# A hybrid decoder step on one core: full-height state products, alternating banks in the chained products, shared sums on two engines

## The chip, the cores and the metric

The kernel runs on one core of one Trainium2 chip. TensorE multiplies matrices out of SBUF into PSUM; VectorE, ScalarE and GpSimd work element by element, and GpSimd does not read PSUM here; transfers are issued by SyncE. The metric is device time in microseconds (us) of one execution, the median of three timed runs. One further execution was taken by the hardware profiler, and all rows below are from it.

## What is computed

One inference step of a two-layer decoder trunk for a prompt of 1,024 tokens, 8 samples of 8 new tokens each, and 16 meta tokens: 1,104 columns, which the kernel keeps with features on the partitions. Layer 0 is a Mamba-2 mixer and an MLP, layer 1 window attention and an MLP. Cut to what the change touches:

```python
# mixer, for each of 8 groups of heads; the samples' chunk is their 8 tokens
chunk_states = jnp.einsum('bclgn,bclgrp->bcgrpn', bb, decay_to_end[..., None] * xdt)
h_new = chunk_decay * h + chunk_states            # h: state_ssm, per sample
...
# MLP of either layer
h + jnp.square(jax.nn.relu(rmsnorm(h, norm_w) @ w_up)) @ w_down
```

All is float32. The kernel reaches that precision by splitting each operand in a rounded high part and the rest (hi and lo, type fp32r) and adding three products, hi·hi, hi·lo and lo·hi.

## The kernel before

**The planner.** The program is written as plain loops over tiles; a planner with a cost model of its own then sets the order of the instructions on each engine's queue and the semaphores. Each engine runs its queue in that order. So the order in the trace is not always that of the loops: where a tile's buffer is not free by the planner's reckoning, it moves another product's matmuls ahead.

**The mixer** (`mixer`, `group_in`, `ssd`; about 17 to 710 us). For each of 8 groups, `group_in` makes four projections of the normed input (`conv_mm`, through `mm3`, lines 179 to 181, into PSUM tiles `g`) for the group after, while `ssd` runs the present group's scan: first the chunk t = 8 (samples and meta tokens), then the prompt's eight chunks. At t = 8 the samples' states are brought forward. The 64 rows are the 8 samples' tokens. `bhl` holds B's hi parts in rows 0 to 63 and its lo parts in rows 64 to 127; `xh` holds x's hi parts in both halves; `bm` is `bhl` masked to one sample's rows, for each of 8 samples. Line 663 multiplies `bm` (128 rows) with `xh`, which gives hi·hi and lo·hi in one; line 664 adds hi·lo with the rows 0 to 63 of `bm` alone and `xl`, a tile of 64 rows from the ring `n1` of five buffers. Both have 256 columns. Line 665 adds two samples' PSUM tile `st` (one buffer) to the states. That is 8 samples in 8 groups, 64 instructions each of lines 663 and 664.

**The chained products** (`up_pair`, about 1,152 to 1,452 and 2,336 to 2,621 us; `down_blocks`, about 1,507 to 1,770 and 2,681 to 2,944 us). The MLP's inner blocks are multiplied by a scheme with seven products for each 2x2 block in place of eight. One chain is seven products; a product i is written in two halves of columns to a pair of PSUM banks, and its pair is named by `CHAIN[i]`, a letter of "adcbacd". There are four pairs, a to d, which is all of PSUM. After each product its pair is read out at once: in `down_blocks` by `tt(to, pv, to)` (line 1056, VectorE) into a target in SBUF. `up` runs 14 chains (f = 2 to 15) in each layer, `down_blocks` 16 (four blocks b, in each four parts p); the next chain begins again with a, then d. So the product 1 of a chain writes to the pair that product 6 of the chain before has left, with the one product 0 between them.

In `down_blocks` the target `uv` collects products that three results share. In the last block (b = 3), behind product 3, line 1081 adds `uv` to three of the four results (`hv[1][1]`, `hv[1][0]`, `hv[0][1]`), all on VectorE: 12 sums in each layer, recorded at line 1056, where `tt` is defined, as hh<-hh,us. Other work on VectorE in that stage: sums of weights (lines 986 and 992) and the lo parts of the next block's activations (line 1024, and line 966 for the block after the chains); on GpSimd the lo parts of the weights (line 856), of which a ring of six holds the parts of six products; on ScalarE the hi parts (lines 855 and 1023).

Of the kernel before, what the change touches and what calls it, by code (L numbers as in the profile page):

```python
# [8 lines left out]
F32 = mybir.dt.float32  # L9
F32R = mybir.dt.float32r  # L10
AF = mybir.ActivationFunctionType
ALU = mybir.AluOpType
# [4 lines left out]
P = 128  # L17
# [124 lines left out]
class Kernel:  # L142
# [180 lines left out]
    def mixer_consts(self, mp):  # L323
        nc, i = self.nc, self.i

        self.tri = mp.tile([P, P], F32, name="tri")
        self.tris = mp.tile([P, P], F32, name="tris")
        self.tri8 = mp.tile([80, 80], F32, name="tri8")
        self.tris8 = mp.tile([80, 80], F32, name="tris8")
        for tl, tls in ((self.tri, self.tris),):  # L330
            nc.gpsimd.memset(tl, 1.0)
            nc.gpsimd.affine_select(out=tl, in_=tl, pattern=[[1, P]], compare_op=ALU.is_ge, fill=0.0, base=0,
                                    channel_multiplier=-1)
            nc.gpsimd.memset(tls, 1.0)
            nc.gpsimd.affine_select(out=tls, in_=tls, pattern=[[-1, P]], compare_op=ALU.is_ge, fill=0.0, base=-1,
                                    channel_multiplier=1)
        for tl, strict in ((self.tri8, False), (self.tris8, True)):
            nc.gpsimd.memset(tl, 1.0)
            sv = tl[:, 0:64].rearrange("s (b q) -> s b q", q=8)
            mv = tl[:, 64:80]  # L340
            if not strict:

                nc.gpsimd.affine_select(out=sv, in_=sv, pattern=[[-8, 8], [0, 8]], compare_op=ALU.is_ge, fill=0.0,
                                        base=0, channel_multiplier=1)
                nc.gpsimd.affine_select(out=sv, in_=sv, pattern=[[8, 8], [1, 8]], compare_op=ALU.is_ge, fill=0.0,
                                        base=0, channel_multiplier=-1)
                nc.gpsimd.affine_select(out=mv, in_=mv, pattern=[[0, 16]], compare_op=ALU.is_ge, fill=0.0, base=-64,
                                        channel_multiplier=1)
                nc.gpsimd.affine_select(out=mv, in_=mv, pattern=[[1, 16]], compare_op=ALU.is_ge, fill=0.0, base=64,
                                        channel_multiplier=-1)  # L350
            else:

                nc.gpsimd.affine_select(out=sv, in_=sv, pattern=[[-8, 8], [-1, 8]], compare_op=ALU.is_ge, fill=0.0,
                                        base=-1, channel_multiplier=1)
                nc.gpsimd.affine_select(out=sv, in_=sv, pattern=[[8, 8], [0, 8]], compare_op=ALU.is_ge, fill=0.0,
                                        base=7, channel_multiplier=-1)
                nc.gpsimd.affine_select(out=mv, in_=mv, pattern=[[-1, 16]], compare_op=ALU.is_ge, fill=0.0, base=-65,
                                        channel_multiplier=1)

        self.bsel = mp.tile([P, NB], F32, name="bsel")  # L360
        nc.gpsimd.memset(self.bsel, 1.0)
        for h in range(2):
            bs = self.bsel[64 * h:64 * h + 64]
            nc.gpsimd.affine_select(out=bs, in_=bs, pattern=[[-8, 8]], compare_op=ALU.is_ge, fill=0.0, base=0,
                                    channel_multiplier=1)
            nc.gpsimd.affine_select(out=bs, in_=bs, pattern=[[8, 8]], compare_op=ALU.is_ge, fill=0.0, base=7,
                                    channel_multiplier=-1)

        self.cv = mp.tile([P, 32, 29], F32, name="cv")
        self.cvo = mp.tile([P, 32, 27], F32, name="cvo")  # L370
        nc.sync.dma_start(out=self.cv, in_=i["cv"])
        nc.scalar.mul(out=self.cv[:, :, 0:5], in_=self.cv[:, :, 0:5], mul=0.5)

        self.dcol = mp.tile([P, 16], F32, name="dcol")
        for h in range(2):
            nc.sync.dma_start(
                out=self.dcol[64 * h:64 * h + 64, :],
                in_=i["a_d_skip"].rearrange("o (t h) -> o h t", h=2)[:, h].broadcast_to([64, 16]),
                allow_slow_non_contiguous=True)
# [170 lines left out]
    def ssd(self, g, fm):  # L550
        nc, i, sp, ps = self.nc, self.i, self.sp, self.psa
# [4 lines left out]
        for t in [8] + list(range(8)):  # L556
# [6 lines left out]
            for h in range(2):  # L563
# [10 lines left out]
                                    in1=hb(self.dt[:n, t, 4 * g:4 * g + 4]), op=ALU.mult)  # L574
# [8 lines left out]
                                    op=ALU.mult)  # L583
# [19 lines left out]
            else:  # L603
# [3 lines left out]
                for b in range(NB):  # L607
                    e = SMP + 8 * b + 8
# [27 lines left out]
            if t == 8:  # L636
                nc.tensor.matmul(out=st[:, 0:256], lhsT=Bt[64:80, :], rhs=xd[64:80], start=True, stop=True)
                hT = sp.tile([P, 256], F32, tag="hT", bufs=2, name="hT")
                nc.vector.tensor_copy(out=hT, in_=st[:, 0:256])

                bhl = sp.tile([P, P], F32R, tag="bhl", bufs=1, name="bhl")
                nc.scalar.copy(out=bhl[:64], in_=Bt[:64])
                nc.vector.tensor_tensor(out=bhl[64:], in0=Bt[:64], in1=bhl[:64].bitcast(F32), op=ALU.subtract)
                xh = sp.tile([P, 256], F32R, tag="xh", bufs=1, name="xdh")
                xl = self.np.tile([64, 256], F32R, tag="n1", bufs=5, name="xdl")
                xdf = xd.rearrange("p h d -> p (h d)")
                nc.scalar.copy(out=xh[:64], in_=xdf[:64])
                nc.scalar.copy(out=xh[64:], in_=xdf[:64])
                nc.vector.tensor_tensor(out=xl, in0=xdf[:64], in1=xh[:64].bitcast(F32), op=ALU.subtract)
                bm = sp.tile([P, NB, P], F32R, tag="bm", bufs=1, name="bm")  # L650
                nc.gpsimd.tensor_tensor(
                    out=bm, in0=bhl.bitcast(F32).rearrange("p (o n) -> p o n", o=1).broadcast_to([P, NB, P]),
                    in1=self.bsel.rearrange("p (b o) -> p b o", o=1).broadcast_to([P, NB, P]), op=ALU.mult)
                hv = h0.rearrange("p b (h d) -> p b h d", d=64)
                for h in range(4):
                    nc.gpsimd.tensor_tensor(
                        out=hv[:, :, h], in0=hv[:, :, h],
                        in1=self.eendb[:, 4 * g + h].rearrange("p (b o) -> p b o", o=1).broadcast_to([P, NB, 64]),
                        op=ALU.mult)
                for b2 in range(4):  # L660
                    sps = ps.tile([P, 2, 256], F32, tag="st", name="st")
                    for b in range(2):
                        nc.tensor.matmul(out=sps[:, b], lhsT=bm[:, 2 * b2 + b], rhs=xh, start=True, stop=False)
                        nc.tensor.matmul(out=sps[:, b], lhsT=bm[:64, 2 * b2 + b], rhs=xl, start=False, stop=True)
                    nc.vector.tensor_tensor(out=h0[:, 2 * b2:2 * b2 + 2], in0=h0[:, 2 * b2:2 * b2 + 2], in1=sps,
                                            op=ALU.add)
                nc.sync.dma_start(out=self.o["ssm_s"][g], in_=h0)
            else:
                nc.tensor.matmul(out=st[:, 0:256], lhsT=Bt, rhs=xd, start=True, stop=True)
                hN = sp.tile([P, 256], F32, tag="hT", bufs=2, name="hT")  # L670
                nc.gpsimd.tensor_tensor(out=hN.rearrange("p (h d) -> p h d", d=64),
                                        in0=hT.rearrange("p (h d) -> p h d", d=64),
                                        in1=hb(self.eend[:, t, 4 * g:4 * g + 4]), op=ALU.mult)
                nc.vector.tensor_tensor(out=hN, in0=hN, in1=st[:, 0:256], op=ALU.add)
                hT = hN
# [80 lines left out]

    CHAIN = "adcbacd"

    def entry(self, big, h_d, w):

# [115 lines left out]
    def up_pair(self, layer, f, rd, rt):  # L878
# [8 lines left out]
        r = self.rx.tile([P, 4, n], F32, tag="rx", bufs=1, name="rx")  # L887

        for i, (wh, wl) in enumerate(self.up_weights(layer, f)):
            b = self.CHAIN[i]  # L890
            first = b not in banks
            if first:
                banks[b] = self.pq.tile([P, 1024], F32, tag=b, bufs=1, name="m" + b)
# [105 lines left out]
    def down_blocks(self, layer, rd, rt, R0, big, c0, chs):  # L999
# [58 lines left out]
        for b in range(4):  # L1058
            for p in range(4):
# [1 line left out]
                hv = [[h[j][i][:, p] for i in range(2)] for j in range(2)]  # L1061
                uv = us[:, p]
                for i, (wh, wl) in enumerate(self.down_weights(layer, b, p)):
                    e = self.CHAIN[i]
                    new = e not in banks
                    if new:
                        banks[e] = pq.tile([P, 1024], F32, tag=e, bufs=1, name="m" + e)
# [8 lines left out]
                        nc.scalar.copy(out=uv, in_=pv)  # L1076
                    else:
                        tt(to, pv, to)
                    if i == 3 and b == 3:
                        for to in (hv[1][1], hv[1][0], hv[0][1]):  # L1080
                            tt(to, to, uv)
                    step(b, p, i)


# [724 lines left out]
```

## Time and profile before

| | us |
|---|---|
| three timed runs, median | 3007.4 |
| their least and greatest | 3004.56, 3008.47 |
| the profiled execution | 3013.72 |
| its span, from the first to the last instruction | 3012.0 |

The profiled execution is 6.3 us longer than the median of the timed runs, and 1.7 us of it lie outside the span. In the span TensorE is busy for 2876.1 us, VectorE for 1963.2, ScalarE for 1453.5, GpSimd for 1397.4. Matmuls are pipelined: one's recorded duration overlaps the next, so what a matmul costs is read from the distance between two starts. A wait is listed with the instruction that waited and the one that released it; "issue" is idle time without a releaser.

### The profile page before, as it was taken

How to read it: one execution, taken by the hardware profiler on the slowest of the kernel's cores; microseconds unless marked ns; L12 is line 12 of the kernel's file. 1: busy time of each engine (PE TensorE's matmuls, PEld its weight loads, DVE VectorE, ACT ScalarE, POOL GpSimd, SP SyncE). 2: the span in 40 equal slices, each digit the busy share in tenths (PEclk: the TensorE clock that was granted, in tenths of full speed). 3: DMA queues.
4: the chain of work that ended last, by engine and by line, in shares of the span. 5: the costliest groups of instructions: out<-in, count | busy, mean ns of one | idle time of the engine just before them, and what ended most of it. 6: DMA issues, size and time to landing. Idle time of an engine off the chain costs nothing.

```text
span 3012.0 us, 50781 instructions
## 1 busy us (share of the span) xinstructions
PE 2876.1 (95%) x19750; PEld 2743.4 (91%) x19750; DVE 1963.2 (65%) x3172; ACT 1453.5 (48%) x2770; POOL 1397.4 (46%) x1231
## 2 busy tenths in 40 slices
PE   5999999999999989999999999999998999999998
PEld 4988898878999989999999999887878999999998
DVE  5777877876565575544467666776779555366675
ACT  5455555545444565444333326556564454433333
POOL 4456665654232305444255555445442544435552
PEclk8999999999999999999999999999998999999998
DMA  3244444445222223444643312223223434443432
GB/s 125 75 112 117 119 120 116 119 133 155 68 69 68 82 79 129 144 145 139 239 142 131 116 50 60 69 71 102 72 94 103 160 131 154 173 176 130 136 101 74
DMA packets 197545, 346.37 MB, mean 115 GB/s; under 512 B 28648, under 2 KB 130920, under 8 KB 194728
## 3 DMA queue, kind: packets, MB, share of 16 engines
q1 hardware_dynamic: 197304, 343.13, 35.7%
q8 instruction: 155, 2.54, 0.3%
q14 instruction: 86, 0.70, 0.1%
HBM read 252.92 MB, written 91.12 MB: 114 GB/s over the span
## 4 chain that ended last, share of the span: by engine, by line
PE 45%; DVE 9%; ACT 4%; issue 3%; POOL 2%; DMA 2%; SPq 0%; DVEq 0%; POOLq 0%; ACTq 0%
PE g L179 3%; PE g L180 3%; PE g L181 3%; PE mc L179 3%; PE mc L181 3%; PE mc L180 3%; PE md L181 3%; PE md L180 3%; PE md L179 3%; PE ma L179 3%; PE ma L181 3%; PE ma L180 3%; PE mb L179 1%; PE mb L180 1%; PE mb L181 1%
## 5 line engine op out<-in xcount | busy, mean ns | idle before, releaser
L179 PE MATMUL g<-S,w 128*128 128x384 f32 (+3 forms) x1656 | 561.3, 339 | 17.5 <-DVE hh L726 4.8
L165 POOL TENSOR_TENSOR w<-raw,w 128x1024 fp32r<-128x1024 f32 x140 | 348.4, 2491 | 475.1 <-ACT w L164 408.1
L180 PE MATMUL g<-S,w 128*128 128x384 f32 (+3 forms) x1656 | 562.8, 340 | 3.6 <-DVE S L319 3.0
L181 PE MATMUL g<-S,w 128*128 128x384 f32 (+3 forms) x1656 | 557.5, 337 | 1.8 <-POOL w L165 1.8
L856 POOL TENSOR_TENSOR w<-s,w 128x384 fp32r<-128x384 f32 (+1 forms) x240 | 326.5, 1363 | 367.0 <-ACT w L855 355.2
L856 POOL TENSOR_TENSOR w<-raw,w 128x384 fp32r<-128x384 f32 (+1 forms) x180 | 222.8, 1240 | 268.0 <-ACT w L855 251.9
L179 PEld LDWEIGHTS g<-S,w 128*128 128x128 f32 (+1 forms) x1656 | 315.1, 190 | 26.2 <-issue 5.9
L180 PEld LDWEIGHTS g<-S,w 128*128 128x128 f32 (+1 forms) x1656 | 315.1, 190 | 10.6 <-DVE S L319 4.1
L181 PEld LDWEIGHTS g<-S,w 128*128 128x128 f32 (+1 forms) x1656 | 315.2, 190 | 8.0 <-issue 3.3
L855 ACT CAST w<-s 128x384 fp32r<-128x384 f32 (+1 forms) x240 | 134.4, 562 | 211.3 <-PE ma L181 69.9
L179 PE MATMUL ma<-S,w 128*128 128x276 f32 (+1 forms) x736 | 212.9, 289 | 5.0 <-DVE us L1056 5.0
L180 PE MATMUL ma<-S,w 128*128 128x276 f32 (+1 forms) x736 | 212.5, 289 | 1.1 <-DVE S L820 0.9
L181 PE MATMUL ma<-S,w 128*128 128x276 f32 (+1 forms) x736 | 212.4, 289 | 0.0
L164 ACT CAST w<-raw 128x1024 fp32r<-128x1024 f32 x140 | 146.5, 1046 | 126.5 <-PE g L180 62.1
L534 DVE SCALAR_TENSOR_TENSOR fm<-xp,cv,fm 128x1024 f32<-128x1024 f32 x96 | 165.4, 1724 | 31.8 <-ACT fm L515 31.2
L855 ACT CAST w<-raw 128x384 fp32r<-128x384 f32 (+1 forms) x180 | 100.6, 561 | 164.0 <-PE md L181 77.3
L726 DVE TENSOR_TENSOR hh<-hh,g 128x384 f32<-128x384 f32 (+2 forms) x264 | 134.1, 530 | 68.8 <-PE g L181 68.3
L179 PE MATMUL md<-S,w 128*128 128x276 f32 (+1 forms) x464 | 135.5, 292 | 8.9 <-DVE hh L1056 8.7
L179 PEld LDWEIGHTS ma<-S,w 128*128 128x128 f32 x736 | 138.6, 188 | 5.7 <-ACT w L855 3.6
L180 PEld LDWEIGHTS ma<-S,w 128*128 128x128 f32 x736 | 138.7, 188 | 1.6 <-DVE S L820 1.1
L181 PEld LDWEIGHTS ma<-S,w 128*128 128x128 f32 x736 | 138.5, 188 | 0.0
L179 PE MATMUL mc<-S,w 128*128 128x276 f32 (+1 forms) x464 | 134.7, 290 | 3.9 <-DVE hh L1056 2.6
(462 smaller groups left out, 8846.6 us busy)
## 6 DMA issues: line engine op xcount, KB each, us to landing
raw<-in_w_up_dram SPq DMA_DIRECT2D x64, 512.0 KB
raw<-in_w_in_dram SPq DMA_DIRECT2D x48, 512.0 KB
raw<-in_w_downs_dram SPq DMA_DIRECT2D x64, 384.0 KB
ab<-acs_d SPq DMA_DIRECT2D x64, 256.0 KB
S<-t_d SPq DMA_DIRECT2D x18, 828.0 KB
S<-t_e SPq DMA_DIRECT2D x18, 816.0 KB
t_d<-rx SPq DMA_DIRECT2D x12, 1104.0 KB
t_e<-rx SPq DMA_DIRECT2D x12, 1088.0 KB
```

What stands on the lines that cost most here:

```text
L164: nc.scalar.copy(out=wh, in_=raw)
L165: nc.gpsimd.tensor_tensor(out=wl, in0=raw, in1=wh.bitcast(F32), op=ALU.subtract)
L179: mm(out=out, lhsT=wh, rhs=xh, start=(first and k == 0), stop=False)
L180: mm(out=out, lhsT=wh, rhs=xl, start=False, stop=False)
L181: mm(out=out, lhsT=wl, rhs=xh, start=False, stop=(k == n - 1))
L534: nc.vector.scalar_tensor_tensor(out=acc[:, :SEQ], in0=xp[:, k:k + SEQ], scalar=cv[:, j, k:k + 1], in1=acc[:, :SEQ], op0=ALU.mult, op1=ALU ...
L726: nc.vector.tensor_tensor(out=hv, in0=hv, in1=pt[:, :n], op=ALU.add)
L855: nc.scalar.copy(out=t[:, 0], in_=src)
L856: nc.gpsimd.tensor_tensor(out=t[:, 1], in0=src, in1=t[:, 0].bitcast(F32), op=ALU.subtract)
```

## The change

Three things change. (1) `xl` becomes a tile of 128 rows that is made once, with zeros in rows 64 to 127; the 64 rows of lo parts are written to its upper half in each group, and line 664's product takes all 128 rows of `bm` and `xl`. (2) `CHAIN` becomes two strings, "adcbacd" for even f or p and "abcdacb" for odd ones: the pairs b and d change places from chain to chain. (3) In the last block of `down_blocks`, the three sums with `uv` are made behind products 3, 4 and 5 in place of all behind 3; the first two, for `hv[1][1]` and `hv[0][1]`, are on GpSimd, the third, for `hv[1][0]`, on VectorE.

```diff
+        self.xl = mp.tile([P, 256], F32R, name="xdl")
+        nc.vector.memset(self.xl[64:].bitcast(F32), 0.0)
...
-                xl = self.np.tile([64, 256], F32R, tag="n1", bufs=5, name="xdl")
+                xl = self.xl
...
-                nc.vector.tensor_tensor(out=xl, in0=xdf[:64], in1=xh[:64].bitcast(F32), op=ALU.subtract)
+                nc.vector.tensor_tensor(out=xl[:64], in0=xdf[:64], in1=xh[:64].bitcast(F32), op=ALU.subtract)
...
                         nc.tensor.matmul(out=sps[:, b], lhsT=bm[:, 2 * b2 + b], rhs=xh, start=True, stop=False)
-                        nc.tensor.matmul(out=sps[:, b], lhsT=bm[:64, 2 * b2 + b], rhs=xl, start=False, stop=True)
+                        nc.tensor.matmul(out=sps[:, b], lhsT=bm[:, 2 * b2 + b], rhs=xl, start=False, stop=True)
...
-    CHAIN = "adcbacd"
+    CHAIN = ("adcbacd", "abcdacb")
...
-            b = self.CHAIN[i]
+            b = self.CHAIN[f % 2][i]
...
-                    e = self.CHAIN[i]
+                    e = self.CHAIN[p % 2][i]
...
-                    if i == 3 and b == 3:
-                        for to in (hv[1][1], hv[1][0], hv[0][1]):
-                            tt(to, to, uv)
+                    if b == 3 and i in (3, 4, 5):
+                        e, to = ((nc.gpsimd, hv[1][1]), (nc.gpsimd, hv[0][1]), (nc.vector, hv[1][0]))[i - 3]
+                        e.tensor_tensor(out=to, in0=to, in1=uv, op=ALU.add)
```

## Rows read from the trace of the kernel before

**Rows 1.** The page's first line and its part 1: the span, and of each engine the busy time, its share of the span and the count of instructions.

```profile
span 3012.0 us, 50781 instructions
...
PE 2876.1 (95%) x19750; PEld 2743.4 (91%) x19750; DVE 1963.2 (65%) x3172; ACT 1453.5 (48%) x2770; POOL 1397.4 (46%) x1231
```

**Rows 2.** Busy time by stretch: the mixer without its ends, the mixer's last group, the chained down products of layer 0, the chained down products of layer 1. Columns: from and to in us, length, then for each engine busy us and the number of instructions, the granted TensorE clock as a share of full speed, the DMA share, GB/s.

```profile
100.00:650.00 550.00, 545.25 (x3576) 489.26 (x3575) 433.88 (x717) 289.09 (x683) 340.72 (x417) 1.00 0.45 118
650.00:710.00 60.00, 49.43 (x313) 39.58 (x313) 43.79 (x90) 32.41 (x75) 36.16 (x37) 0.91 0.43 107
...
1507.00:1770.00 263.00, 253.86 (x1965) 251.55 (x1963) 178.49 (x203) 91.72 (x134) 141.03 (x109) 0.99 0.35 117
...
2681.00:2944.00 263.00, 253.68 (x1993) 251.68 (x1991) 177.40 (x203) 93.99 (x138) 138.63 (x109) 0.99 0.36 122
```

**Rows 3.** The longest of TensorE's waits in the mixer, 100 to 650 us: who waited for whom, us in total, times, longest one.

```profile
PE st L663 <- POOL bm L651: 2.0, 2, 1.0
```

**Rows 4.** TensorE's instructions in order of time, in group 0 (146 to 149 us) and in group 7 (from 680 us): start, duration, engine, line, operation, out and in, rows*columns of the weights, shape of the moving operand, count. How far apart two starts are is what one matmul costs the engine; the durations overlap.

```profile
146.48 0.32 PE L181 MATMUL g<-S,w 128*128 128x336 f32 x1
146.72 0.38 PE L664 MATMUL st<-xdl,bm 64*128 64x256 f32 x1
147.04 0.38 PE L663 MATMUL st<-xdh,bm 128*128 128x256 f32 x1
147.35 0.38 PE L664 MATMUL st<-xdl,bm 64*128 64x256 f32 x1
147.66 0.42 PE L179 MATMUL g<-S,w 128*128 128x336 f32 x1
...
148.23 0.34 PE L179 MATMUL g<-S,w 128*128 128x384 f32 x1
148.40 0.33 PE L180 MATMUL g<-S,w 128*128 128x384 f32 x1
...
680.62 0.38 PE L664 MATMUL st<-xdl,bm 64*128 64x256 f32 x1
680.94 0.66 PE L596 MATMUL y<-dec,xdt 128*64 128x128 f32 x8
```

**Rows 5.** The same view inside a product of the second layer's up stage.

```profile
2400.35 0.29 PE L180 MATMUL ma<-S,w 128*128 128x272 f32 x1
2400.48 0.29 PE L181 MATMUL ma<-S,w 128*128 128x272 f32 x1
```

**Rows 6.** All matmuls of line 664: count, least, median and greatest duration in ns, first and last start in us, form.

```profile
L664 PE MATMUL st<-xdl,bm x64: 377/381/388, 146.7 to 680.6; 64*128 64x256 f32 x64
```

**Rows 7.** TensorE's waits in the chained down products of layer 0 (the first four rows), of layer 1 (the next two) and in the up products of layer 0 (the last; the same view of layer 1's up products, 2336 to 2625 us, has no row).

```profile
PE md L179 <- DVE hh L1056: 3.7, 2, 2.3
PE ma L179 <- DVE us L1056: 3.2, 2, 1.6
PE mc L179 <- DVE hh L1056: 1.3, 2, 0.6
PE g L179 <- DVE hh L1056: 0.9, 1, 0.9
...
PE md L179 <- DVE hh L1056: 5.0, 2, 2.7
PE ma L179 <- DVE us L1056: 1.7, 2, 1.1
...
PE mc L179 <- DVE rx L885: 1.4, 1, 1.4
```

**Rows 8.** TensorE's instructions in order of time where the last block (b = 3) of layer 0's chained down products begins, and then the same place of layer 1; in brackets the idle time before one and what ended it.

```profile
1708.89 0.40 PE L179 MATMUL md<-S,w 128*128 128x276 f32 x1 [2.30 <-DVE hh L1056]
...
1712.31 0.43 PE L180 MATMUL md<-S,w 128*128 128x276 f32 x1
1712.54 0.43 PE L181 MATMUL md<-S,w 128*128 128x276 f32 x1
...
1716.62 0.36 PE L179 MATMUL md<-S,w 128*128 128x276 f32 x1 [1.36 <-DVE hh L1056]
...
2881.41 0.39 PE L179 MATMUL md<-S,w 128*128 128x272 f32 x1 [2.32 <-DVE hh L1056]
...
2889.41 0.36 PE L179 MATMUL md<-S,w 128*128 128x272 f32 x1 [2.69 <-DVE hh L1056]
```

**Rows 9.** Busy time by stretch, as in rows 2, for two short stretches after those waits.

```profile
1708.90:1712.70 3.80, 3.80 (x18) 3.80 (x19) 3.80 (x3) 0.00 (x0) 2.75 (x2) 0.57 0.00 0
...
2889.40:2893.70 4.30, 4.29 (x23) 4.30 (x24) 4.30 (x9) 1.03 (x2) 1.50 (x2) 0.62 0.00 0
```

**Rows 10.** VectorE's instructions in order of time at the same place of layer 0 (b = 3 begins).

```profile
1692.15 1.88 DVE L1024 TENSOR_TENSOR A<-A 128x1656 fp32r<-128x1656 f32 x1 [0.81 <-ACT A L1023]
...
1717.50 2.18 DVE L1056 TENSOR_TENSOR hh<-hh,us 128x552 f32<-128x552 f32 x2
...
1726.93 0.73 DVE L1056 TENSOR_TENSOR hh<-md,hh 128x552 f32<-128x552 f32 x1 [1.55 <-PE md L181]
```

**Rows 11.** Instructions of lines 1056, 986 and 856 in layer 0's chained down products, columns as in rows 6.

```profile
L1056 DVE TENSOR_TENSOR hh<-hh,us x12: 716/729/1539, 1717.5 to 1764.7; 128x552 f32<-128x552 f32 x12
...
L986 DVE TENSOR_TENSOR s<-raw x28: 543/550/1376, 1513.7 to 1737.5; 128x384 f32<-128x384 f32 x28
...
L856 POOL TENSOR_TENSOR w<-s,w x61: 1004/1017/2658, 1506.4 to 1756.5; 128x384 fp32r<-128x384 f32 x61
```

## The prediction, made before the changed kernel was run

> **What bounds the kernel now.** I read the engine totals first: TensorE is busy for 95% of the span, VectorE for 65%, GpSimd for 46% [rows 1]. So an edit pays where it takes time out of TensorE's stream, and nowhere else unless it ends a wait of TensorE. Then I read the three places that the change touches, each by its own stretch [rows 2]. In the mixer TensorE is busy for 545.25 of 550 us, VectorE for 433.88, GpSimd for 340.72. Its longest wait there comes to 2.0 us in all [rows 3]. The reader is to see a stage that is nothing but TensorE's stream, with a fifth of VectorE's time left over. The mixer's last group is different: 49.43 of 60 us at a granted clock of 0.91, with no projections left to fill in. In the chained down products TensorE is busy for 253.86 and 253.68 of 263 us, so some 9 us in each layer are waits [rows 2].
>
> A busy TensorE is not one at its peak, so I read the distance between starts next. In a stream of equal shape, 272 columns take 0.13 us [rows 5] and 384 take 0.17 [rows 4]; on that line 256 columns take 0.12. Around line 664 they take 0.31 to 0.32: 146.72, 147.04, 147.35, 147.66 [rows 4]. The odd one there is the height: 64 rows of weights between neighbours of 128. Recorded durations hide it, 0.38 us for both lines. TensorE counts as busy all the while, so no list of waits shows it.
>
> Last, the waits of the chained products [rows 7]. The up products have one of 1.4 us in layer 0 and none in layer 1. In the down products TensorE waits for VectorE's read-outs: 3.7 us on pair d, 3.2 on a, 1.3 on c in layer 0, and 5.0 on d, 1.7 on a in layer 1.
>
> **Part 1, the full-height products.** Added: one memset of 64 rows by 256 at the start, beside loads; nothing waits for it but the first product of line 664, at 146.7 us [rows 6]. The write of `xl` on VectorE stays as it is. Its tile no longer takes one of five buffers of the ring n1, which can only free others. As `xl` is one tile now, its write in a group waits for line 664 of the group before, some 75 us past (seven groups from 146.7 to 680.6 [rows 6]). No column is added: line 664 streams 256 columns as before. What goes is the change of height on both sides of each line 664. There are 64 [rows 6], each with a way in and a way out at 0.31 in place of 0.12: 64 x 2 x 0.19 = 24.3 us. This is the upper bound. Some ways out lead to line 596, whose weights are 64 columns wide (680.62 to 680.94 [rows 4]); that is a change of shape of its own and stays in part. So I take 22 us of TensorE's stream.
>
> How much of it reaches the end? Seven of eight groups, 19.3 us, lie where TensorE is busy for 99% of the time. With the stage shorter by 19 us, VectorE would be busy for 434 of 531, 82%, still not the bound, though some of its reads will come due too late. I take 0.9 of it, 17.4 us. The last group's 2.8 us lie in the scan's serial chain, beside idle time; I take half, 1.4. Sum 18.8 us. Lower bound 10: half swallowed by VectorE and by the order that the planner now finds. Can the part cost time? Only if a product of 64 rows were cheaper where it stands, and rows 4 show none that is.
>
> The Trainium skill speaks on both sides of this. TensorEngine Tiling (Array Packing), Key Properties, says that going from one tiling mode to another drains TensorE; the rows' 0.31 us agree. The same page under When to Use Tiling counsels the reverse of this change, that contractions of at most 64 rows be run as half-height tiles, since two such tiles can run side by side. By that rule padding would throw time away; it is the fifth rival below.
>
> **Part 2, the pairs of banks.** In the chain's own order, product 1 of a chain needs the pair d that product 6 of the chain before has just left, with one product (18 matmuls of some 0.13, 2.3 us) for VectorE to read it out. Now product 1 takes the pair that product 3 of the chain before left, four products earlier; product 3 takes that of product 6, three products earlier. Within a chain nothing changes: a is used again after three products, c after two. So the shortest distance between chains goes from one product to two (product 4 to the next product 0).
>
> In the up products the planner has already moved other matmuls ahead and TensorE does not wait [rows 7], so I take 0 there, with -1.4 as the best.
>
> In the down products the waits on d are four: 2.30 and 1.36 us in layer 0, 2.32 and 2.69 in layer 1 [rows 8], all where b = 3 begins. The first of each is product 1 behind product 6, 4.6 us in all; it should go. The second is product 6 behind the read-out of product 1 in the same chain, 4.05 us; it comes earlier when product 1 does, but is not lifted by the new letters. Behind the waits the granted clock is 0.57 and 0.62 [rows 9], near the lower of the two levels (1.2 GHz), after TensorE had stood idle for 2.3 to 2.7 us: in layer 0, 17 distances in 3.65 us (1708.89 to 1712.54 [rows 8]) in place of 2.2, a loss of 1.4; in layer 1 a loss of about 1.3. Together 4.6 + 4.05 + 2.7 = 11.4 us. Against taking all of it: VectorE works without a break from 1692.15 until the idle 1.55 us before 1726.93 [rows 10], so a read-out that no longer blocks one product will be late for another. I take half, 5.5. At the end of the chains, the first product of the next block waits 0.9 us for the last read-out of d [rows 7], in either layer by my estimate; the last chain (p = 3) now ends on b. Which bank that product takes is not to be seen before; half of 1.8, 0.9. Part 2 is 6.4 us, between 0 and 11.4 + 1.8 = 13.2.
>
> **Part 3, the shared sums.** 24 sums at 0.73 us [rows 11] are on VectorE; 16 of them leave, 11.7 us. But VectorE is idle between read-outs for most of b = 3 (1.55 us before 1726.93 [rows 10]); only the first chain's two per layer fall into the busy run, where two took 2.18 us at 1717.50 [rows 10]. GpSimd has no such sum in the trace. Nearest is line 856, 384 columns in 1.00 us undisturbed and 2.66 at most [rows 11]; 552 columns would be 1.44 to 3.8. Queued behind a sum on GpSimd are the lo parts of later weights (line 856), and TensorE waits for these; the cover is the ring of six products' parts. Behind the sum for `hv[0][1]` waits VectorE's read-out of product 6, and with it its queue; the cover is products 4 and 5, 4.6 us. GpSimd is busy for 141.03 of 263 us [rows 2]. I take 0, between -2 (the busy run) and +3. The +3 comes from a neighbour on VectorE that is slowed: line 986 goes from 0.55 to 1.38 us [rows 11], 0.83 for each of the two sums in the first chain of either layer.
>
> Here a rule speaks against the change as well. SBUF — State Buffer, Who interferes with whom, in the Trainium skill: a VectorE instruction with two SBUF inputs and a GpSimd one that reads SBUF block each other, and the second waits for the whole of the first. Rows 11 agree, with 0.55 to 1.38 and 1.00 to 2.66. Sums from SBUF on GpSimd then still take VectorE's time.
>
> **The sum.** 18.8 + 6.4 + 0 = 25.2 us off. Against the profiled execution's 3013.7 us this gives 2988.5. That execution is 6.3 above the median; against the median of 3007.4 it is **2982**.
>
> **The rivals.**
> First, only the mixer pays: VectorE's busy run, not the banks, sets the waits of the down products. For it: 33 us without a break. 3007.4 - 18.8 = 2989.
> Second, both pay in full: 24.3 + 13.2 off, 2970. For it: TensorE's 99% in the mixer. Against it: the busy run.
> Third, the mixer's gain is mostly swallowed, because VectorE's and GpSimd's work comes due late when TensorE runs ahead (5 us are left): 3007.4 - 5 - 6.4 = 2996. Against it: 82% at most.
> Fourth, the change does not do what it says: the 0.31 us come from something else than the height, say from the change between operands, and stay. 3007.4 - 6.4 = 3001. Against it: the streams of rows 5 change operands in every matmul at 0.13.
> Fifth, a half-height product costs TensorE almost nothing beside its neighbours, and padded it costs its 0.12 us: 64 x 0.12 = 7.7 slower, less 6.4, 3009. Against it: the 0.31 us after each. It is the rule on half-height tiles above.
> Sixth, slower: GpSimd becomes the bound of the last block. One chain gives TensorE 7 x 18 x 0.126 = 15.9 us. GpSimd has seven of line 856 in it, at the stage's mean of 1.29 us (141.03 / 109 [rows 2]) 9.1, and two sums, 2.9: 12.0, which fits. It decides when line 856 takes over (15.9 - 2.9) / 7 = 1.86 us there. At 2.0 with sums of 3.8 it is 21.6, 5.7 too much in each of 8 chains: 3007.4 - 18.8 + 46 = 3035.
>
> **How the numbers follow.** What a measurement of this kernel can tell from no change is about 0.2%, 6 us: below 3001.4 is faster, above 3013.4 slower. Chances: forecast 0.46, only the mixer 0.20, both in full 0.10, mixer swallowed 0.10, no effect of the height 0.05, half-height cheaper 0.03, GpSimd the bound 0.06. The first four are faster, 0.86; the next two within, 0.08; the last slower, 0.06. The range ends at both bounds: 24.3 + 13.2 + 2 off gives 2968, and 10 off with nothing from the banks and 3 for the sums gives 3000.
>
> **What the profile after would show.** Starts of lines 663 and 664 some 0.12 us apart, the form of line 664 128*128, the stretch from the first projections to the last scan shorter by 17 to 20 us; the waits of md on hh at the start of b = 3 gone or below 1 us, the clock there at 1.00; the up stages as long as before within 2 us; hh<-hh,us on GpSimd at 1.4 to 2.7 us and no wait of VectorE on it. Wrong would be: starts still 0.3 apart, or VectorE waiting for GpSimd before product 6's read-out, or the planner's new order putting gaps into the up stages, which have none now.

## The result and the profile after

The changed kernel takes 2987.2 us, median of four runs (2977.05 to 2988.97), beside 3007.6 for the kernel before: a ratio of 0.9927, 95% interval 0.9903 to 0.9951. Timed once more beside the experiments, it came to 0.9912 (0.9896 to 0.9928). The forecast was 2982, so 0.9915. The profiled execution took 2977.05 us.

The page's first line and part 1 of the changed kernel, which answer to [rows 1]:

```profile
span 2975.3 us, 50874 instructions
...
PE 2842.1 (96%) x19750; PEld 2728.4 (92%) x19750; DVE 1956.7 (66%) x3157; ACT 1455.1 (49%) x2770; POOL 1424.9 (48%) x1247
```

The same number of matmuls; TensorE is busy for 34 us less, GpSimd for 27.5 more. Where the time came from is read by stage. Each time below is the distance between matmuls that mark a stage's ends in the profiled execution: the scan to the last start of the prompt's state product (line 669 before), the chained stages from the first to the last start of matmuls into the pairs a to d.

| us | before | after |
|---|---|---|
| start to the end of the scan | 708.5 | 686.8 |
| from there to the first up chain | 443.2 | 443.4 |
| up chains, layer 0 and layer 1 | 300.2, 305.5 | 301.1, 304.7 |
| down chains, layer 0 | 268.9 | 266.4 |
| end of these to the up chains of layer 1 (attention) | 555.4 | 545.1 |
| down chains, layer 1 | 265.0 | 263.6 |
| what follows them | 69.3 | 68.1 |

The scan gave 21.7 us, the down chains and what follows 5.1, the up chains nothing. The 10.3 us of the attention stage are not the change's: no instruction is changed there, and the granted clock differs from execution to execution. The stage in the busy time by stretch, of the kernel before and then of the changed one (the two numbers before the last two are the clock and the DMA share):

```profile
1769.00:2325.00 556.00, 519.56 (x3408) 475.45 (x3407) 416.36 (x925) 312.91 (x744) 269.50 (x220) 0.95 0.26 79
```

```profile
1746.00:2291.00 545.00, 508.49 (x3404) 464.59 (x3404) 417.39 (x926) 312.37 (x744) 271.04 (x220) 0.98 0.26 81
```

By the clock, 0.05 x 556 = 28 us of full speed are missing in the one and 0.02 x 545 = 11 in the other; not all of that is on the path. In a second profile of the changed kernel (e9) the stage took 553.1 us and the whole execution 2988.6. So some 26 of the 36.7 us between the two profiled spans are the change's own, and the rest is put down to the attention stage's clock.

TensorE's order of time in group 1 of the changed mixer, to be held against [rows 4]. Line 666 was 663, and 667 was 664:

```profile
212.91 0.34 PE L180 MATMUL g<-S,w 128*128 128x384 f32 x1
213.08 0.28 PE L666 MATMUL st<-xdh,bm 128*128 128x256 f32 x1
213.20 0.28 PE L667 MATMUL st<-xdl,bm 128*128 128x256 f32 x1
213.32 0.28 PE L666 MATMUL st<-xdh,bm 128*128 128x256 f32 x1
213.44 0.28 PE L667 MATMUL st<-xdl,bm 128*128 128x256 f32 x1
213.55 0.34 PE L181 MATMUL g<-S,w 128*128 128x384 f32 x1
```

The starts stand 0.12 us apart, where they stood 0.31. Summed over all 128 state products, the distance to the next start fell from 37.8 to 17.6 us.

That is not the whole gain, since a change of height also lengthened the matmul behind it. The kernel before, behind the last half-height product of group 0 in [rows 4]:

```profile
147.66 0.42 PE L179 MATMUL g<-S,w 128*128 128x336 f32 x1
147.92 0.31 PE L180 MATMUL g<-S,w 128*128 128x336 f32 x1
148.07 0.32 PE L181 MATMUL g<-S,w 128*128 128x336 f32 x1
```

The first of these takes 0.26 us to the next start, the second, of the same shape, 0.15. So I also summed TensorE's whole stream from the first state product to the end of the scan, without its idle time: 550.7 us before and 525.5 after. The clock has a part in this: TensorE stood at the 1.2 GHz level for 10.2 us of that stretch before and for 6.8 after. In e7 and e11, two runs described below with the same mixer, it stood there for 10.2 us as before, and the stream is 526.4 and 526.3. So at the same clock the stream shrank by some 24 us. The idle time in the stretch grew from 15.3 to 19.3 us.

The longest of TensorE's waits in the changed mixer, and then in the down chains of layer 0 and of layer 1, which answer to [rows 3, 7]:

```profile
PE st L666 <- POOL bm L654: 7.3, 4, 2.7
```

```profile
PE mb L179 <- DVE hh L1059: 3.3, 1, 3.3
PE ma L179 <- DVE us L1059: 2.2, 2, 1.3
...
PE mb L179 <- DVE hh L1059: 2.6, 1, 2.6
```

The reader is to see that the wait on pair d has become one on pair b: product 3 of the first chain of b = 3 now waits for the read-out of product 6 before it, which is on b. In both layers together 8.7 us on d have become 5.9 us on b. And in the mixer a small wait has grown, 2.0 to 7.3 us, for `bm`. What TensorE did around that wait on b:

```profile
1681.59 0.28 PE L181 MATMUL mc<-A,w 128*128 128x276 f32 x1
1685.16 0.57 PE L179 MATMUL mb<-A,w 128*128 128x276 f32 x1 [3.28 <-DVE hh L1059]
1685.52 0.43 PE L180 MATMUL mb<-A,w 128*128 128x276 f32 x1
1685.75 0.43 PE L181 MATMUL mb<-A,w 128*128 128x276 f32 x1
```

After 3.28 us of idleness the starts stand 0.23 apart in place of 0.13, as they did in [rows 8]. The sums on GpSimd, to be held against [rows 11]:

```profile
L1084 POOL TENSOR_TENSOR hh<-hh,us x16: 1357/1378/1694, 1694.8 to 2902.9; 128x552 f32<-128x552 f32 x8, 128x544 f32<-128x544 f32 x8
```

### The profile page after: what moved, and what is told of

Its sections match the earlier page's. It is cut to its first block, busy times and chain, and to the rows that moved or that the text cites. A ratio compares the mean times of both kernels' runs of the same rounds, so it can differ in the third digit from the quotient of the medians.

```text
span 2975.3 us, 50874 instructions
## 1 busy us (share of the span) xinstructions
PE 2842.1 (96%) x19750; PEld 2728.4 (92%) x19750; DVE 1956.7 (66%) x3157; ACT 1455.1 (49%) x2770; POOL 1424.9 (48%) x1247
## 4 chain that ended last, share of the span: by engine, by line
PE 46%; DVE 9%; ACT 4%; issue 3%; POOL 2%; DMA 1%; DVEq 0%; SPq 0%; POOLq 0%; ACTq 0%
PE g L179 4%; PE g L180 3%; PE g L181 3%; PE mc L179 3%; PE mc L181 3%; PE mc L180 3%; PE ma L179 3%; PE ma L180 3%; PE ma L181 3%; PE md L181 2%; PE md L180 2%; PE mb L179 2%; PE mb L180 2%; PE md L179 2%; PE mb L181 2%
## 5 line engine op out<-in xcount | busy, mean ns | idle before, releaser
L179 PE MATMUL mc<-S,w 128*128 128x276 f32 (+1 forms) x464 | 134.4, 290 | 2.7 <-DVE rx L888 1.4
L181 PE MATMUL mc<-S,w 128*128 128x276 f32 (+1 forms) x464 | 134.0, 289 | 0.0
```

What stands on the lines that cost most here:

```text
L179: mm(out=out, lhsT=wh, rhs=xh, start=(first and k == 0), stop=False)
L181: mm(out=out, lhsT=wl, rhs=xh, start=False, stop=(k == n - 1))
```

## The experiments

The theory: (1) TensorE pays about 0.19 us for each change between 64 and 128 rows of weights, 128 times, and these lie in its stream; (2) in the down chains VectorE's unbroken run sets the waits, and the letters of the banks choose where they fall; (3) the sums are covered. The main rival for (1): the gain comes from the buffer of the ring n1 that `xl` frees, and the order that the planner then finds. Edits are against the kernel before unless said otherwise; each kernel is timed beside the kernel before on the same chip. Ratios have their 95% interval; the stages, in us, are each from one profiled execution.

| run | ratio | scan | down chains, layer 0 and 1 |
|---|---|---|---|
| before | 1 | 708.5 | 268.9, 265.0 |
| changed kernel, again (e9) | 0.9912 (0.9896 to 0.9928) | 689.0 | 265.5, 263.3 |
| e1, part 1 alone | 0.9925 (0.9910 to 0.9939) | 686.8 | 268.5, 264.9 |
| e2, part 2 alone | 0.9964 (0.9951 to 0.9977) | 709.6 | 264.4, 263.2 |
| e3, part 3 alone | 0.9990 (0.9979 to 1.0001) | 710.9 | 271.1, 266.3 |
| e4, own tile of 64 rows | 1.0013 (1.0000 to 1.0025) | 717.7 | 271.4, 264.7 |
| e5, half of the changes of height | 0.9960 (0.9949 to 0.9972) | 697.4 | 270.8, 266.5 |
| e8, parts 1 and 2 | 0.9913 (0.9899 to 0.9927) | 691.7 | 265.0, 263.9 |
| e6, e8 and bm first | 0.9909 (0.9893 to 0.9926) | 680.8 | 272.4, 264.8 |
| e7, e8 and lo parts on GpSimd | 0.9918 (0.9901 to 0.9936) | 687.4 | 266.5, 266.1 |
| e11, e8 and lo parts late | 0.9903 (0.9889 to 0.9917) | 687.6 | 258.9, 260.5 |
| e12, e11 and bm first | 0.9893 (0.9874 to 0.9911) | 682.2 | 265.8, 262.1 |
| e13, e12 with the lo parts placed | 0.9870 (0.9853 to 0.9887) | 682.1 | 264.3, 260.2 |

The stages differ somewhat between executions of the same instructions: the scan ends at 686.8 to 691.7 us in the six profiles with the changed mixer that do not make `bm` first, and the down chains of layer 0 take 268.5 to 271.4 us in the four that leave them as they were.

**Each part alone.** e1, e2 and e3 are the three parts of the diff, one at a time.

> Part 1 alone on the kernel before: full-height tile with zeros, nothing else. Height theory (each change of height on TensorE costs about 0.19 us, 128 of them in TensorE's stream): the scan's end moves up by 19 to 23 us and the time falls by 18 to 22 us, most of the whole change's 20. Rival, the down products pay: the time falls by under 12 us and parts 2 and 3 hold the rest.

> Part 2 alone: the pairs b and d change places. If the banks set the waits: the wait of product 1 where b = 3 begins goes in both layers, 5 to 9 us faster with the clock kept. If VectorE's unbroken run sets them: the wait comes back on another pair within a product or two, 0 to 4 us faster. The mixer stays as before within 2 us in both.

> Part 3 alone: two of three shared sums on GpSimd. If they are covered: within 3 us of before. If VectorE's run is the bound at the start of b = 3: up to 3 us faster. If GpSimd becomes the bound of the last block: slower by 5 us or more, with VectorE or TensorE waiting for GpSimd there.

Part 1 alone ends the scan at 686.8 us, as the whole change does, and leaves every chained stage within 0.6 us. So the mixer's 21.7 us are part 1's. Part 2 alone takes 6.3 us out of the down chains and 1.2 out of what follows; by its ratio it is 10.9 us faster (6.9 to 14.8). TensorE's wait for the read-out of d is gone, and one stands on b. The order of time in e2, where b = 3 of layer 0 begins:

```profile
1706.16 0.37 PE L179 MATMUL mb<-A,w 128*128 128x276 f32 x1 [3.04 <-DVE hh L1056]
1706.37 0.29 PE L180 MATMUL mb<-A,w 128*128 128x276 f32 x1
1706.50 0.29 PE L181 MATMUL mb<-A,w 128*128 128x276 f32 x1
...
1713.07 0.40 PE L180 MATMUL md<-S,w 128*128 128x276 f32 x1 [1.52 <-DVE S L1024]
```

That is neither of the two expectations whole: the wait does come back, at product 3 in place of product 1 and longer, but the starts behind it are 0.13 us apart, at full clock, and d has no second one for a read-out (what ends the 1.52 us is a lo part, line 1024). By the stages the gain is 7.5 us, more than the 0 to 4 of the second expectation. Part 3 alone made the down chains 3.5 us longer in its profile, and its ratio does not tell it from no change; e5, which leaves these stages alone, has them 3.4 us longer, so this is no more than executions differ by. In no profile does VectorE wait for a sum on GpSimd.

**Height or buffer.** e4 takes `xl` out of the ring but leaves its height; e5 leaves ring and shapes and halves the changes of height.

```diff
+        self.xl = mp.tile([64, 256], F32R, name="xdl")
...
-                xl = self.np.tile([64, 256], F32R, tag="n1", bufs=5, name="xdl")
+                xl = self.xl
```

> The kernel before with the lo parts of x in a tile of their own, still of 64 rows, so that the ring of five buffers has one user less and the product keeps its height. Height theory: starts of lines 663 and 664 stay 0.31 us apart, time within 4 us of before. Ring theory (the gain of part 1 comes from the freed buffer and the order that the planner then finds): 10 us faster or more.

```diff
                     for b in range(2):
-                        nc.tensor.matmul(out=sps[:, b], lhsT=bm[:, 2 * b2 + b], rhs=xh, start=True, stop=False)
-                        nc.tensor.matmul(out=sps[:, b], lhsT=bm[:64, 2 * b2 + b], rhs=xl, start=False, stop=True)
+                        nc.tensor.matmul(out=sps[:, b], lhsT=bm[:, 2 * b2 + b], rhs=xh, start=(b == 0), stop=False,
+                                         skip_group_check=True)
+                    for b in range(2):
+                        nc.tensor.matmul(out=sps[:, b], lhsT=bm[:64, 2 * b2 + b], rhs=xl, start=False, stop=(b == 1),
+                                         skip_group_check=True)
```

> The kernel before with the four products of a pair of samples in another order: both of line 663, then both of 64 rows. The same instructions with the same shapes, but half of the changes of height (64 in place of 128). Height theory: 64 x 0.19, so 9 to 12 us faster, the scan's end earlier by as much. Rival, a product of 64 rows costs 0.31 us by itself whatever stands beside it: within 3 us of before.

The freed buffer alone gains nothing, 1.0013. Its scan is 9.2 us longer, and that is mostly the clock: over 100 to 650 us the granted clock is 0.98, where it was 1.00 [rows 2]. TensorE stood at the 1.2 GHz level for 17 us there, each time behind a wait for `bm`, which loses 8.5 us. The busy time by stretch of e4:

```profile
100.00:650.00 550.00, 542.73 (x3519) 488.08 (x3518) 414.48 (x698) 283.86 (x667) 336.42 (x410) 0.98 0.43 116
```

The planner's order did change, though: the wait for `bm` is 7.3 us in e4 too, so it comes with the own tile and not with the height. With half of the changes of height the scan ended 11.1 us earlier, and TensorE's stream in it, without idle time and with as much time at 1.2 GHz as before, is 538.8 us (550.7 before, some 526.4 with none). Halving the count halves the cost: 11.9 us for 64 changes, 24.3 for 128, 0.19 each. In e5's order of time two products of 64 rows side by side take 0.43 us to the next start, where each alone took 0.31, so the price is not the 64-row product's own:

```profile
146.15 0.50 PE L666 MATMUL st<-xdl,bm 64*128 64x256 f32 x2
146.58 0.42 PE L181 MATMUL g<-S,w 128*128 128x336 f32 x1
146.84 0.32 PE L179 MATMUL g<-S,w 128*128 128x336 f32 x1
146.99 0.32 PE L180 MATMUL g<-S,w 128*128 128x336 f32 x1
```

Here too the matmul behind them takes 0.26 us in place of 0.15. So a change of height lengthens both of its neighbours: by some 0.09 us the matmul in front of it (0.12 to 0.21 at the median for a state product) and by some 0.10 the one behind. A half-height product between two full ones has a change on either side, which makes its 0.31.

**What the parts make together.** e8 is the changed kernel with the sums as before; e9 is the changed kernel itself.

> The changed kernel without its part 3: full-height products and alternating pairs, the shared sums on VectorE as before. If the parts add up: the sum of parts 1 and 2 alone, 0.9885 to 0.9895 of before, and 2 to 4 us below the changed kernel, since part 3 alone made the down products longer by 3.5 us. If part 3 is neutral or helps once the banks alternate: the same as the changed kernel within 2 us, 0.9925 to 0.994.

> The changed kernel itself, on the chip and beside the runs that the next two are read against. Parts add up: 0.99 to 0.991 of before. As in its first timing: 0.9925 to 0.994. In its profile the time by stage again: scan about 687 us, chained down products about 266 and 264 us, attention between 545 and 555 us, with the granted clock of that execution.

0.9913 and 0.9912, with down chains of 265.0 and 263.9 us against 265.5 and 263.3: part 3 makes no difference once the banks alternate. Both ratios lie between the two ranges that were expected. The parts' ratios multiply to 0.9879, with an interval of some 0.0022 either way if the three are independent, and e9's interval begins at 0.9896. So that something is lost in the whole is not shown; by stage nothing is, 21.7 + 7.5 - 3.5 = 25.7 us for the parts beside some 26 for the whole.

**Which wait stands in the down chains.** e7 moves the lo parts of the block behind the chains (line 969 in these files) from VectorE's run to GpSimd; e11 keeps them on VectorE, but behind the read-outs.

```diff
-        nc.vector.tensor_tensor(out=lo, in0=lo.bitcast(F32), in1=hi.bitcast(F32), op=ALU.subtract)
+        (e or nc.vector).tensor_tensor(out=lo, in0=lo.bitcast(F32), in1=hi.bitcast(F32), op=ALU.subtract)
...
-                    self.block_parts(p - 1, R0)
+                    self.block_parts(p - 1, R0, nc.gpsimd)
...
```

> Parts 1 and 2, and the lo parts of the block behind the chains (four instructions in each layer, 1.3 to 2.1 us each, in VectorE's unbroken run where b = 3 begins) on GpSimd. If VectorE's run sets the waits there: the run is 5 to 7 us shorter and TensorE's wait on the pair b falls from 2.6 to 3.3 us to under 1.5 in both layers, 3 to 6 us below parts 1 and 2. If GpSimd's work in turn makes the weights' lo parts late, or its sharing with VectorE slows both: within 2 us or slower.

```diff
-                    self.block_parts(p - 1, R0)
+                    with self.tc.issue_after(self.last_read):
+                        self.block_parts(p - 1, R0)
                 if p == 3 and i == 5:
-                    self.block_parts(3, R0)
+                    with self.tc.issue_after(self.last_read):
+                        self.block_parts(3, R0)
...
-                        tt(to, pv, to)
+                        self.last_read = tt(to, pv, to).ins
```

> Parts 1 and 2, and the lo parts of the block behind the chains stay on VectorE but are queued behind the read-out of the step that the loop puts them in, so that the planner can no longer draw them ahead to where b = 3 begins. Takes some 6.5 us out of VectorE's unbroken run there and adds no work to any engine. If VectorE's run sets the waits there: TensorE's wait on the pair b falls from 3.3 and 2.6 us to under 1 us, the stages from 265 and 264 us to about 261. If something else sets them (the parts of the activations, their transfers): the wait stays over 2 us and the stages within 1.5 us.

e7 gained nothing: TensorE still waits for a read-out, in layer 0 on b and in layer 1 on c, 5.8 us at once. Its longest wait in the down chains of either layer:

```profile
PE mb L179 <- DVE hh L1059: 3.2, 1, 3.2
...
PE mc L179 <- DVE hh L1059: 7.5, 5, 5.8
```

The orders of time of VectorE and then GpSimd in layer 0 of e7 show what VectorE did meanwhile:

```profile
1679.38 5.74 DVE L989 TENSOR_TENSOR s<-raw 128x384 f32<-128x384 f32 x2
1685.04 0.72 DVE L1059 TENSOR_TENSOR hh<-mb,hh 128x552 f32<-128x552 f32 x1
```

```profile
1679.00 5.71 POOL L969 TENSOR_TENSOR R<-R 128x1104 fp32r<-128x1104 f32 x2
```

Two sums that take 0.55 us each undisturbed [rows 11] take 5.74 together, as long as GpSimd's two lo parts beside them. The work left VectorE's queue and came back as longer sums. e11, which adds no work anywhere, does what the theory says. TensorE's waits in its down chains of layer 0:

```profile
PE ma L179 <- DVE us L1061: 2.2, 2, 1.1
PE g L180 <- DVE R L969: 2.1, 1, 2.1
```

No wait on b is left in either layer, and the stages are 6.1 and 3.4 us shorter than in e8. So VectorE's run was the bound there. Part of it is given back: the lo parts now come late for the block behind the chains, 2.1 us in each layer. The time of the whole, 0.9903, is not told from e8's 0.9913; the gain is read from the stages alone.

**A faster version.** e6 queues the scaling of the states behind `bm` on GpSimd; e12 is e11 with that; e13 places the lo parts between the two extremes.

```diff
-                nc.gpsimd.tensor_tensor(
+                made = nc.gpsimd.tensor_tensor(
                     out=bm, in0=bhl.bitcast(F32).rearrange("p (o n) -> p o n", o=1).broadcast_to([P, NB, P]),
...
-                for h in range(4):
+                with self.tc.issue_after(made.ins):
+                    for h in range(4):
...
```

> Parts 1 and 2, and GpSimd makes the masked copies bm before it scales the states (the scaling is queued behind bm). In the changed kernel TensorE waits 7.3 us in the mixer for bm, which stands behind the four scalings, 2.0 us in the kernel before. If that wait is on the path: 4 to 8 us below parts 1 and 2 without it. If what stands behind it is late anyway (the states' scaled tiles for line 668): within 2 us.

> Parts 1 and 2, the lo parts late as in the run before, and bm made before the states are scaled. If both moves hold: scan at about 681 us, chained down products at about 261 us in both layers, 8 to 14 us below the changed kernel. If the stage after takes the gain back, as the down products of layer 0 did in the run with bm first alone: within 3 us of the run before.

```diff
-                if p > 0 and i == 2:
+                if p in (1, 2) and i in (2, 5):
                     with self.tc.issue_after(self.last_read):
-                        self.block_parts(p - 1, R0)
-                if p == 3 and i == 5:
-                    with self.tc.issue_after(self.last_read):
-                        self.block_parts(3, R0)
+                        self.block_parts(2 * p - 2 + i // 5, R0)
```

> As the run before, but the four lo parts are queued behind products 2 and 5 of the second and third chain (p = 1, 2) of the last block in place of products 2 of the second to fourth and 5 of the fourth. Where they were, the last of them was late for the block behind the chains: TensorE waited 2.1 us for it in each layer. If that is all: 3 to 5 us below the run before, 0.987 to 0.989 of the kernel before, with no wait on the pair b and none on the lo parts. If they come early enough to fall into VectorE's unbroken run again: the wait on b is back at 1 us or more and the time within 2 us of the run before.

With `bm` first the scan ends at 680.8 us, 6.0 before the changed kernel's, and TensorE's wait for `bm` is gone. The whole is no faster than e8 (0.9909 and 0.9913): the down chains of layer 0 take 272.4 us in e6, 7.4 more than in e8, although VectorE and GpSimd run the same instructions in the same order there. TensorE is idle for 11.7 us in them in place of 7.3, and stands at 1.2 GHz for 6.8 us, in e8 for none. VectorE's waits for activations in that stage, of e8 and then of e6:

```profile
DVE R L1027 <- ACT R L1026: 5.4, 2, 4.4
```

```profile
DVE R L1028 <- ACT R L1027: 8.3, 3, 4.4
```

ScalarE waits in turn for the transfers of these activations, and they land later relative to TensorE's stream. That this is the cause is read from the waits and was not tested, nor why they land later. The stage is longer in e12 and e13 as well (265.8 and 264.3 against e11's 258.9), so e12 reaches its 8 to 14 us (9.7 below the changed kernel) without the 261 us that were expected of that stage. e13 has no wait on b and none for the lo parts, and is the fastest kernel of the study: 2975.8 us, 0.9870; its interval ends at 0.9887, below the 0.9896 where that of the changed kernel's second timing begins.

## Why the prediction was right

**Part 1, 18.8 us forecast, 21.7 measured** (e1: 0.9925, some 22 us). The mechanism was right: 128 changes of height at 0.19 us. The term that was too low is TensorE's stream: 22 us were taken, and it shrank by some 24 at the same clock, which is the whole of the 24.3 that was called the upper bound. The share of it that reached the scan's end, 0.85 in the sum (18.8 of 22), is about what came: 21.1 of some 25 us, since idle time grew by 4.0. But what took it back is not what the forecast named. VectorE did not come late; the wait for `bm` on GpSimd grew by 5.3 us, while other waits fell a little. It comes from the planner's order (e4) and cost about 6 us (e6). That term was not in the sum: an edit that only takes a tile out of its ring moved GpSimd's queue. Up to 1.7 us of the 21.7 are the clock, which happened to stand at 1.2 GHz for a shorter time. The fourth rival is refuted by the starts, 0.12 us apart, and by e5. So is the fifth: e5's 0.43 us for two half-height products are twice the 0.12 of any product of 256 columns and 0.19 for the change. Two half-height products that run at the same time were not tried.

**Part 2, 6.4 us forecast, 7.5 measured** alone (e2, by stage), 5.1 in the whole. By e2's ratio it is 10.9 us (6.9 to 14.8), so the forecast may be low. That VectorE's run keeps a part is what the runs show: the wait of 2.30 and 2.32 us on d came back as 3.3 and 2.6 on b, and e11 lifts it. That the part is a half was a guess between 0 and 13.2 us (and half of 11.4 is 5.7, not 5.5); that it came near is luck. What was wrong is what the profile after was to show: I had written that the clock there would be at 1.00 and the wait below 1 us; the wait is as long, there is only one in place of two, and in the profiled execution the clock still falls behind it in both layers (in e2, e8 and e9 only in layer 1). The end of the chains gave 1.2 us in layer 1, where half of 1.8 in all was taken; layer 0's wait of 0.9 us there is gone as well, in time that the table counts to the attention stage.

**Part 3, 0 us forecast, between -2 and +3**: 0.999 alone, and 0.9913 against 0.9912 with and without it. A sum takes 1.38 us on GpSimd, just below the 1.44 to 3.8 that were worked out. The sixth rival did not occur. Sums that went to GpSimd still took VectorE's time, as the prediction said: 11.7 us of them left VectorE, and its busy time fell by only 3.3 us from before to e3 and by 2.0 from e8 to e9 (two profiles of the changed kernel differ by 3.8).

**The up chains**, taken at 0, are within 0.9 us of before in both layers, although the planner gave them a new order.

**The sum**, 25.2 us, stands beside 22 by the ratio of the first timing (14.7 to 29.2 by its interval) and 26.5 by that of the second (21.7 to 31.3), and beside 26.4 in the profiles without the attention stage. The time alone does not tell the first rival from the forecast: 2987.2 us in the first timing lies nearer to its 2989 than to 2982. The stages and e2 do it: the mixer paid nearly in full, and the banks, which by that rival give nothing, by about half. That the sum came out nearer than its terms is in part luck as well, since part 1 gave 2.9 us more than forecast and part 2, in the whole, 1.3 less.

## What to carry to other kernels

Read the distance between matmul starts, not the list of waits: an engine that pays at every change of weight height is busy throughout and waits for nothing, and 64 rows of zeros were then cheaper here than a half-height matmul between full ones. Sum the stream on both sides of the change, since its neighbours pay too. Before giving a waiting product another bank, look at what the reading engine does in those microseconds; if it works without a break, much of the wait only changes its name (8.7 us on d, 5.9 on b), and what helped here was to move work out of that run in time, not to an engine beside whose instructions its own took longer. Expect a planner to find another order after any edit, and compare by stage, so that a stage that was not touched can be set aside.

## What the runs showed of the hardware that was not expected

The spread between executions of one kernel (2977 to 2994 us for the changed one in its two timings) goes with the granted clock of the whole execution, 0.984 to 0.986 in the three fastest and 0.977 to 0.981 in the others. In the two that were profiled, most of the difference (8.0 of 11.6 us) is in the attention stage, which no run changed. Over the profiles of runs with part 1 that stage took between 543.6 us (e7) and 555.9 us (e13) for the same work; in e11 and e12 it also has the wait for late lo parts. TensorE fell to the 1.2 GHz level there behind short idle stretches, none over 5 us, and not at the same places in each execution: in the changed kernel's profile five times, 23.8 us in all, in e13's six times, 51 us. The same wait need not have the same effect: behind the 2.7 us wait for `bm` in the mixer the clock fell for 6.8 us in e4 and 3.4 in e9, and not at all in the first profile of the changed kernel.

And the sharing between VectorE and GpSimd goes further than the rows of before showed: the same sum that went from 0.55 to 1.38 us at most [rows 11] took 2.87 in e7 (5.74 for two) beside a GpSimd instruction of that length.
